# Seven contraction blocks of a modulation moved from VectorE to row products on TensorE, in the prologue of a hybrid decoder block

## The chip, the core and the metric

One core of one Trainium2 chip runs the whole kernel. The metric is the device time of one execution in microseconds (us). The kernel before takes 1734.45 us, the median of three runs that lie between 1732.58 and 1735.91 us.

## What is computed

A decoder block for 1024 tokens of width 1024, in float32. The input is normalised by RMS and modulated by a vector computed from a conditioning vector `c`; then come two mixers (a gated convolution and an mLSTM), a merge, an output projection and a SwiGLU feed-forward part. What matters here is the very beginning:

```python
mod = jnp.einsum("bd,de->be", jax.nn.silu(c), w_ada[l]) + b_ada[l]
sh1, sc1, g1, sh2, sc2, g2 = jnp.split(mod[:, None, :], N_MOD, axis=-1)

h = rms_norm(x, norm_mix_g[l]) * (1.0 + sc1) + sh1
proj = jnp.einsum("bsd,de->bse", h, w_in[l]) + b_in[l]
```

So nothing of the first projection can start before `sh1` and `sc1` are there for the channels that it contracts over, and these are two vectors of 1024 sums over 1024 terms each, that is 8 MB of `w_ada`.

## The kernel before

**The main part.** Matrix products are made from float32 numbers split in two: a high part rounded to fp32r (`hh`, `whi`) and the rest (`hl`, `wlo`), so a product is three fp32r products: high by high, high by low, low by high. After the prologue TensorE works through blocks of 128 output channels; line 158 is the product of such a block. VectorE runs convolution taps and splits beside it.

**The prologue** (lines 175 to 380) prepares `hh` and `hl`, the modulated input in transposed form, channels on partitions: eight tiles `hh[k]` and `hl[k]` of 128 channels by 1024 tokens. The steps:

1. SyncE issues the loads, in this order: the input `x` (4 MB), the first group of `w_ada` (`wad[0]`, four pieces of 512 KB), two raw weight matrices of the first two output blocks (`wraw`, 512 KB each), then the other three groups of `w_ada`.
2. Line 235 squares `x` on ScalarE for the RMS, line 244 scales `x`. Line 248 transposes it on TensorE in 16 blocks of four 128x128 pieces: eight channel tiles `k` for the first half of the tokens (q = 0), then eight for the second half (q = 1). A block lands in one of three PSUM buffers, one of the kind `pn` and two of the kind `pc`. Line 251 copies it out to `xT[k]`, by the string `EVAC` either on ScalarE ("a": all eight of the first half, five of the second) or on VectorE ("v": `xT1`, `xT4`, `xT7` of the second half). The next block that uses the buffer has to wait for that copy.
3. The modulation is made in four groups of 256 channels, `g` = 0 to 3. `mod_sums(g)` forms on VectorE, in eight dependent steps (line 275, then line 277 seven times), the sum over the eight blocks `k` of `wad[g][:, k]` times the column `sc_c[:, k]` of silu(c); the result `macc` still has 128 partial sums, on the partitions. `mod_products(g)` (line 283) adds these up on TensorE: four float32 products of a 128x128 piece of `macc` with a column of ones, into the PSUM buffer `pa`.
4. `mod_cols(g)` (lines 292 and 293) makes columns of `sh1` and `G1` from them on ScalarE. Line 297 makes `hh[k]` for the two tiles of the group, line 300 the full-precision value in place, both on ScalarE, and line 336 makes `hl[k]` from the two on VectorE. For the last group VectorE makes the full value itself (line 340).
5. `first_products(g, kind)` (line 308) multiplies the group's two tiles into the first two output blocks `first[0]` and `first[1]`; the split weights of these are `w_first` (`wf` in the profile), split by `split_rest()` with line 148 (high part, ScalarE) and line 149 (low part, VectorE). For a group there are 16 products with `hh` (`kind` 0: high and low weights) and 8 with `hl` (`kind` 1).
6. After the last group, `glu_gate` reads `first[0]` (line 412, ScalarE), and the next output block at line 158 takes over its PSUM buffer. Four transposes of parameter rows (line 125, through the one buffer `pa`) stand on TensorE around the last products.

**What sets the order.** Every engine runs its instructions strictly in the order of its own program. That order is made when the kernel is built, by a scheduler that goes by priorities (the order in the source) and by its own estimate of when each operand will be there. `in_turn` ties down part of it: the groups in the lists `on_v` (VectorE), `on_s` (ScalarE) and `on_t` (TensorE) stay in the order of the list. The two splits of `split_rest()`, and the copies of the first half of the tokens, stand in no such list.

Of the kernel before, what the change touches and what calls it, by code (L numbers as in the profile page):

```python
# [8 lines left out]
F32 = mybir.dt.float32  # L9
F32R = mybir.dt.float32r  # L10
I32 = mybir.dt.int32
AF = mybir.ActivationFunctionType
# [5 lines left out]
KT = 8  # L18
# [18 lines left out]
EVAC = ("aaaaaaaa", "avaavaav")  # L37
KX = 6
MACC = 3
XB = 7  # L40
GLU_B = 1024
Q0, K0, V0, O0 = 2048, 3072, 4096, 5120
# [6 lines left out]
def hybrid_block(ctx: ExitStack, tc: tile.TileContext, x, c, w_ada, b_ada, norm_mix_g, w_in, b_in,  # L49
                 conv_dw_w, conv_dw_b, conv_ln_g, conv_ln_b, w_conv_pw, b_conv_pw, qk_conv_w,  # L50
                 qk_conv_b, mlstm_norm_g, w_out, norm_ffn_g, w_ffn_up, w_ffn_down, final_norm_g, out):
    nc = tc.nc
# [11 lines left out]
    def ps_mm():  # L64
        return ps.tile([128, 2, 512], F32, name="mm", bufs=2)

    def ps_a():
        return ps.tile([128, 512], F32, name="pa", bufs=1)

    def ps_n():  # L70
        return ps.tile([128, 512], F32, name="pn", bufs=1)

    def ps_c():
        return ps.tile([128, 512], F32, name="pc", bufs=2)
# [20 lines left out]
    ones_col = const.tile([128, 1], F32, name="ones_col")  # L95
# [56 lines left out]
    HALVES = ((0, 512), (512, 1024))  # L152
# [17 lines left out]
    def flat(t):  # L170
        return t.rearrange("p a b -> p (a b)")
# [6 lines left out]
    hh = [big.tile([128, S], F32R, name=f"hh{k}", tag="xa") for k in range(KT)]  # L178
# [5 lines left out]
    pro = prologue.enter_context(tc.tile_pool(name="pro", bufs=1, reuse_waits="tile"))  # L184
    rows = pro.tile([128, 8, 128], F32, name="rows", tag="rows", bufs=2)
    param_columns(param_rows(1, [("c", as_rows(c, 8), 8)], rows[:, 0]))
    sc_c = const.tile([128, KT], F32, name="sc_c")
# [6 lines left out]
    wad = []  # L194
# [35 lines left out]
    rstd = pro.tile([128, 3, 8], F32, name="rstd")  # L230
    xT = [big.tile([128, S], F32, name=f"xT{k}", tag="xb") if k < XB else pro.tile([128, S], F32, name=f"xT{k}") for k in range(KT)]
    for q in range(2):
# [12 lines left out]
        for k in range(KT):  # L245
            p = ps_n() if k % 3 == 0 else ps_c()
# [3 lines left out]
            e = "s" if EVAC[q][k] == "a" else "v"  # L250
            ins = nc.scalar.activation(h, p, AF.Copy) if e == "s" else nc.vector.tensor_copy(h, p)
# [18 lines left out]
    def mod_sums(g):  # L270
        acc = pro.tile([128, 2, 256], F32, name="macc", tag="macc", bufs=MACC)
        parts = [[], []]
        for k in range(KT):
            if k < 1:
                ins = nc.vector.tensor_scalar(acc, wad[g][:, k], sc_c[:, k:k + 1], None, op0=OP.mult)
            else:
                ins = nc.vector.scalar_tensor_tensor(acc, wad[g][:, k], sc_c[:, k:k + 1], acc, op0=OP.mult, op1=OP.add)
            parts[k // 4].append(ins)
        return acc, parts

    def mod_products(g, acc):
        p = ps_a()
        out = [nc.tensor.matmul(p[:, i:i + 1], acc[:, i // 2, (i % 2) * 128:(i % 2) * 128 + 128], ones_col, start=True, stop=True)
               for i in range(4)]
        return p, out

    def mod_cols(g, p):
# [14 lines left out]
    def first_products(g, kind):  # L302
        ks = (2 * g, 2 * g + 1)
        x = hl if kind else hh
        steps = [(i, k, n) for n in ((0,) if kind else (0, 1)) for k in ks for i in range(2)]
        if g == 3 and kind:
            steps.sort(key=lambda step: step[0])
        return [nc.tensor.matmul(flat(first[i])[:, a:b], w_first[i][n][:, k, :], x[k][:, a:b],
                                 start=(g == 0 and k == 0 and n == 0 and not kind), stop=(g == 3 and k == KT - 1 and kind == 1))
                for i, k, n in steps for a, b in HALVES]  # L310

    on_v, on_s, on_t = [], [], []
    w_next = [None]
    hl = []
    acc, parts = mod_sums(0)
    on_v.append(parts[1])
    on_v.append(late_evac["v"])
    on_s.append(late_evac["s"])
    split_rest()
    p, ins = mod_products(0, acc)  # L320
    for g in range(4):
        on_s.append(mod_cols(g, p))
        ks = (2 * g, 2 * g + 1)
# [3 lines left out]
        if g < 3:  # L327
            acc, parts = mod_sums(g + 1)
            on_v += parts
        else:  # L330
            w_next[0] = wp.tile([128, KT, 128], F32R, name="whi", tag="whi"), wp.tile([128, KT, 128], F32R, name="wlo", tag="wlo")
            raw_next = load_raw(win, 0, KT, GLU_B + 128)
# [12 lines left out]
        if g == 2:  # L345
# [10 lines left out]
            bif = const.tile([128, 8], F32, name="bif")  # L356
            nc.sync.dma_start(bif, bass.AP(tensor=b_in.tensor, offset=b_in.offset + IF0, ap=[[0, 128], [1, 8]]))
        on_t.append(first_products(g, 0))
        if g < 3:
            p, ins = mod_products(g + 1, acc)  # L360
            on_t.append(ins)
        on_t.append(first_products(g, 1))
    for groups in (on_v, on_s, on_t):
        in_turn([x for x in groups if x])
# [400 lines left out]
    def chain(*gens):  # L765
        for g in gens:
            yield from g
# [168 lines left out]
    p = ps_a()  # L936
# [25 lines left out]
    def kx(name):  # L962
        return up_.tile([128, D], F32, name=name, tag="kx", bufs=KX)
# [236 lines left out]
    steps = chain(*(w_out_part(q, eh, xs, ss, banks(n)) for n, (q, eh, xs, ss) in  # L1200
                    enumerate(((0, 0, xs0, ss0), (0, 1, xs0, ss0), (1, 0, xs1, ss1), (1, 1, xs1, ss1)))))
# [84 lines left out]
    for gidx, nf in enumerate(groups):  # L1286
# [4 lines left out]
        for t in range(8):  # L1291
# [3 lines left out]
            if gidx < 3:  # L1295
                p = ps_mm()
# [40 lines left out]
```

## Time and profile before

| | before |
|---|---|
| median of three runs | 1734.45 us |
| the profiled execution: its time, and the span from its first instruction to its last | 1735.88 us, 1734.1 us |
| TensorE busy | 1692.9 us, 98% of the span |
| TensorE weight loads | 1418.6 us, 82% |
| VectorE busy | 1249.7 us, 72% |
| ScalarE busy | 611.7 us, 35% |
| GpSimd busy | 52.7 us, 3% |

Times in the rows are counted from the start of the span. PE is TensorE, PEld its weight loads, DVE VectorE, ACT ScalarE, POOL GpSimd, SP SyncE. A row of the timeline gives start, duration, engine, line and operation, out<-in, shapes and a count; several instructions of one kind in succession are one row, and the duration is then that of all. The bracket at the end is idle time of the engine just before, and what ended it.

### The profile page before, as it was taken

To read this page: it belongs to the slowest core of one execution; us is meant where nothing else is said; L and a number is where in the kernel's file an instruction comes from. 1 tells how busy PE (TensorE), PEld (TensorE's weight loads), DVE (VectorE), ACT (ScalarE), POOL (GpSimd) and SP (SyncE) were. 2 spreads that over 40 slices of the span, in tenths; PEclk is the share of its full clock that TensorE was granted. 3 is DMA by queue.
4 is the path that set the end of the run, shared out by engine and by line. 5 is a ranking of instruction groups with operands and counts; after the bars stand their busy time and mean duration, and the time that the engine had idled before them with its cause. 6 is when DMAs were issued, how large, how long until landed. Compare 5 with 4: busy or idle time off the path is not lost. (4 is left out here: it accounts for less than half of the span.)

```text
span 1734.1 us, 20875 instructions
## 1 busy us (share of the span) xinstructions
PE 1692.9 (98%) x8360; PEld 1418.6 (82%) x8360; DVE 1249.7 (72%) x1681; ACT 611.7 (35%) x809; POOL 52.7 (3%) x113
## 2 busy tenths in 40 slices
PE   5999999999999999999999998999999999999998
PEld 4788889888988888888888778888888888778887
DVE  6989998997799669446798668766666665685243
ACT  7424335323433253223522386322222222232122
POOL 0000001000001000000000000000000000000000
PEclk9999999999999999999999999999999999999999
DMA  9221120221111112243694743322222222653121
GB/s 320 63 62 49 37 71 28 61 73 49 37 49 61 61 49 61 73 146 98 209 376 167 230 152 104 98 86 85 86 73 75 84 81 96 226 168 101 58 94 52
DMA packets 194711, 179.91 MB, mean 104 GB/s; under 512 B 7463, under 2 KB 166711, under 8 KB 194615
## 3 DMA queue, kind: packets, MB, share of 16 engines
q1 hardware_dynamic: 177367, 146.61, 27.4%
q10 hardware_dynamic: 17248, 31.99, 5.0%
q8 instruction: 65, 1.06, 0.3%
q14 instruction: 31, 0.25, 0.0%
HBM read 146.06 MB, written 32.51 MB: 103 GB/s over the span
## 5 line engine op out<-in xcount | busy, mean ns | idle before, releaser
L388 DVE SCALAR_TENSOR_TENSOR cacc<-a,col,cacc 128x1024 f32<-128x1024 f32 x240 | 306.8, 1286 | 3.9 <-ACT cacc L386 1.4
L158 PE MATMUL mm<-hh,wlo 128*128 128x512 f32 x864 | 271.2, 391 | 1.5 <-DVE wlo L149 1.5
L158 PE MATMUL mm<-hl,whi 128*128 128x512 f32 x864 | 272.5, 392 | 0.0
L158 PE MATMUL mm<-hh,whi 128*128 128x512 f32 x864 | 271.6, 392 | 0.0
L158 PEld LDWEIGHTS mm<-hh,wlo 128*128 128x128 f32 x864 | 160.3, 188 | 33.6 <-DVE wlo L149 2.7
L158 PEld LDWEIGHTS mm<-hl,whi 128*128 128x128 f32 x864 | 161.0, 188 | 32.1 <-issue 0.5
L158 PEld LDWEIGHTS mm<-hh,whi 128*128 128x128 f32 x864 | 160.5, 188 | 31.6
L148 ACT ACTIVATE whi<-wraw 128x1024 fp32r<-128x1024 f32 x61 | 64.7, 1061 | 226.5 <-PE mm L158 171.3
L149 DVE TENSOR_TENSOR wlo<-wraw,whi 128x1024 fp32r<-128x1024 f32 x61 | 74.5, 1222 | 28.7 <-ACT whi L148 25.2
L1114 PE MATMUL mm<-Bh,gh 128*128 128x512 f32 (+1 forms) x192 | 71.5, 375 | 2.9 <-ACT gh L1051 1.5
L1115 PE MATMUL mm<-Bl,gh 128*128 128x512 f32 (+1 forms) x192 | 71.5, 373 | 0.6 <-DVE Bl L1033 0.6
L604 PE MATMUL mm<-wlo,hh 128*128 128x256 f32 x256 | 72.0, 282 | 0.0
L1116 PE MATMUL mm<-Bh,gl 128*128 128x512 f32 (+1 forms) x192 | 71.2, 371 | 0.0
L1303 DVE TENSOR_TENSOR x<-x,mm 128x1024 f32<-128x1024 f32 x24 | 29.3, 1219 | 52.0 <-PE mm L1301 49.6
L1179 ACT ACTIVATE whi<-wraw 128x512 fp32r<-128x512 f32 (+2 forms) x32 | 25.3, 792 | 114.8 <-PE mm L1301 75.8
L535 DVE SCALAR_TENSOR_TENSOR cacc<-qkraw,col,cacc 128x1024 f32<-128x1024 f32 x48 | 61.5, 1282 | 4.9 <-ACT cacc L533 4.5
L603 PE MATMUL mm<-whi,hh 128*128 128x256 f32 x192 | 54.6, 284 | 0.0
L605 PE MATMUL mm<-whi,hl 128*128 128x256 f32 x192 | 54.2, 283 | 0.0
L1299 PE MATMUL mm<-fa,whi 128*128 128x512 f32 x128 | 50.6, 396 | 1.6 <-DVE cu L1142 0.9
L1300 PE MATMUL mm<-fa,wlo 128*128 128x512 f32 x128 | 50.5, 395 | 1.2 <-DVE wlo L1180 1.2
L1301 PE MATMUL mm<-fa,whi 128*128 128x512 f32 x128 | 50.6, 395 | 0.0
L1052 DVE TENSOR_TENSOR ul<-uraw,uh 128x1024 fp32r<-128x1024 f32 x20 | 24.5, 1225 | 35.4 <-ACT uh L1051 35.4
(444 smaller groups left out, 3893.1 us busy)
## 6 DMA issues: line engine op xcount, KB each, us to landing
wraw<-in_w_in_dram SPq DMA_DIRECT2D x64, 512.0 KB
awt<-in_w_ada_dram SPq DMA_DIRECT2D x32, 512.0 KB
graw<-in_w_ffn_up_dram SPq DMA_DIRECT2D x24, 512.0 KB
uraw<-in_w_ffn_up_dram SPq DMA_DIRECT2D x22, 512.0 KB
draw<-in_w_ffn_down_dram SPq DMA_DIRECT2D x22, 512.0 KB
act_d<-cg ACTq DMA_DIRECT2D x38, 256.0 KB
wad<-in_w_ada_dram SPq DMA_DIRECT2D x16, 512.0 KB
wraw<-in_w_out_dram SPq DMA_DIRECT2D x16, 512.0 KB
```

Source lines behind the costliest of these rows:

```text
L148: nc.scalar.activation(hi, raw, AF.Copy)
L149: (eng or nc.vector).tensor_sub(lo, raw, hi.bitcast(F32))
L158: nc.tensor.matmul(flat(acc)[:, a:b], lhs[:, k, :], rhs[k][:, a:b], start=(first and k == 0), stop=(last and k == kt - 1))
L388: nc.vector.scalar_tensor_tensor(acc, a[:, j:j + S], dw_col(j, ct), acc, op0=OP.mult, op1=OP.add)
L535: nc.vector.scalar_tensor_tensor(cv, raw[:, j:j + S], wcol(j), cv, op0=OP.mult, op1=OP.add)
L603: nc.tensor.matmul(o, hh[k][:, ts_], his[k], start=False, stop=False)
L604: nc.tensor.matmul(o[:, 0:256], hh[k][:, ts_], los[k], start=False, stop=False)
L605: nc.tensor.matmul(o, hl[k][:, ts_], his[k], start=False, stop=(k == KT - 1))
L1114: nc.tensor.matmul(o, a, rh, start=(k == 0), stop=False)
L1115: nc.tensor.matmul(o, a, rl, start=False, stop=False)
L1116: nc.tensor.matmul(o, b, rh, start=False, stop=(k == 3))
L1299: nc.tensor.matmul(o, hi[:, i, :], his[i][:, a:b], start=(i == 0), stop=False)
```

## The change

`ROWS = (3, 4, 0, 0)` gives for each group the number of contraction blocks that leave VectorE. For these blocks TensorE multiplies directly: the column `sc_c[:, k]` is the stationary operand and the 512 numbers per partition of `wad[g][:, k]` are the moving one, so that a float32 product of 1x512 adds up the partitions at once, in one PSUM row (`pa` for group 0, a `pc` buffer for group 1). ScalarE copies the row to SBUF (new line 281). `mod_products` then needs, for each of the four pieces, one more product that turns a piece of the row into a column (new line 299), which the old product with ones (new line 300) adds to. VectorE has five blocks left in group 0 and four in group 1. Group 1's row products are tied into the order of TensorE, and its copy into that of ScalarE; group 0's are not.

`first_products` hands out the last group's 24 products in another order of the source: first those with high parts, without the low weights of the second block; then the `hl` products of the first block; then the rest of the second block.

```diff
+ROWS = (3, 4, 0, 0)
...
     def mod_sums(g):
         acc = pro.tile([128, 2, 256], F32, name="macc", tag="macc", bufs=MACC)
         parts = [[], []]
-        for k in range(KT):
-            if k < 1:
+        row, ins = None, []
+        if ROWS[g]:
+            p = (ps_c() if g else ps_a())[0:1, :]
+            for k in range(ROWS[g]):
+                ins.append(nc.tensor.matmul(p, sc_c[:, k:k + 1], wad[g][:, k].rearrange("p i e -> p (i e)"),
+                                            start=(k == 0), stop=(k == ROWS[g] - 1)))
+            row = pro.tile([1, 512], F32, name="macc", tag="macc", bufs=MACC)
+            copied = nc.scalar.activation(row, p, AF.Copy)
+            (on_t if g else []).append(ins)
+            (on_s if g else []).append([copied])
+        for k in range(ROWS[g], KT):
+            if k == ROWS[g]:
...
-    def mod_products(g, acc):
+    def mod_products(g, sums):
+        acc, row = sums
         p = ps_a()
-        out = [nc.tensor.matmul(p[:, i:i + 1], acc[:, i // 2, (i % 2) * 128:(i % 2) * 128 + 128], ones_col, start=True, stop=True)
-               for i in range(4)]
+        out = []
+        for i in range(4):
+            o = p[:, i:i + 1]
+            if row is not None:
+                out.append(nc.tensor.matmul(o, row[:, i * 128:(i + 1) * 128], ones_col[0:1, :], start=True, stop=False))
+            out.append(nc.tensor.matmul(o, acc[:, i // 2, (i % 2) * 128:(i % 2) * 128 + 128], ones_col, start=row is None, stop=True))
         return p, out
...
-        steps = [(i, k, n) for n in ((0,) if kind else (0, 1)) for k in ks for i in range(2)]
-        if g == 3 and kind:
-            steps.sort(key=lambda step: step[0])
+        steps = [(i, k, n, x) for n in ((0,) if kind else (0, 1)) for k in ks for i in range(2)]
+        if g == 3:
+            if not kind:
+                return []
+            high = [(i, k, n, hh) for n in (0, 1) for k in ks for i in range(2) if n == 0 or i == 0]
+            steps = high + [s for s in steps if s[0] == 0] + [(1, k, 1, hh) for k in ks] + [s for s in steps if s[0] == 1]
```

Three places in the programs that the engines get show what the builder makes of it. First ScalarE, from the scaling of the last part of `x` to the second-half copies, before; `xT4` to `xT7` with the sources `pc_194` to `pc_212` are the last four copies of the first half, `wf00` and `wf10` the splits of the two raw matrices:

```order
L242 ACTIVATE xt3_110<-xt3_110,rstd_147 128x1024
L251 ACTIVATE xT3_151<-pn_188 128x512
L251 ACTIVATE xT4_152<-pc_194 128x512
L251 ACTIVATE xT5_153<-pc_200 128x512
L251 ACTIVATE xT6_154<-pn_206 128x512
L251 ACTIVATE xT7_155<-pc_212 128x512
L148 ACTIVATE wf00_124<-wraw_126 128x1024
L251 ACTIVATE xT0_148<-pn_232 128x512
L148 ACTIVATE wf10_128<-wraw_130 128x1024
L251 ACTIVATE xT2_150<-pc_244 128x512
```

The same place now, where `macc_291` is the row of group 0:

```order
L243 ACTIVATE xt3_110<-xt3_110,rstd_147 128x1024
L252 ACTIVATE xT3_151<-pn_188 128x512
L149 ACTIVATE wf00_124<-wraw_126 128x1024
L281 ACTIVATE macc_291<-pa_287 1x512
L149 ACTIVATE wf10_128<-wraw_130 128x1024
L252 ACTIVATE xT4_152<-pc_194 128x512
L252 ACTIVATE xT5_153<-pc_200 128x512
L252 ACTIVATE xT6_154<-pn_206 128x512
L252 ACTIVATE xT7_155<-pc_212 128x512
L252 ACTIVATE xT0_148<-pn_232 128x512
L252 ACTIVATE xT2_150<-pc_244 128x512
```

Both splits and the copy of the row now stand ahead of four copies that they followed. On VectorE, in the same stretch, the low part of the first split (`wf01`, which needs `wf00`) now comes ahead of all sums of group 0, and the second one behind the first of them; before, they stood behind the sixth and the seventh of eight. The next place on ScalarE is that of the first two `hh` tiles; before, from there to the columns of group 1:

```order
L297 ACTIVATE hh0_82<-xT0_148,sh1_91,G1_90 128x1024
L297 ACTIVATE hh1_83<-xT1_149,sh1_91,G1_90 128x1024
L300 ACTIVATE xT0_148<-xT0_148,sh1_91,G1_90 128x1024
L300 ACTIVATE xT1_149<-xT1_149,sh1_91,G1_90 128x1024
L292 ACTIVATE sh1_91<-pa_341,mod_b_282 128x1
```

And now, where `macc_325` is the row of group 1:

```order
L313 ACTIVATE hh0_82<-xT0_148,sh1_91,G1_90 128x1024
L313 ACTIVATE hh1_83<-xT1_149,sh1_91,G1_90 128x1024
L281 ACTIVATE macc_325<-pc_320 1x512
L316 ACTIVATE xT0_148<-xT0_148,sh1_91,G1_90 128x1024
L316 ACTIVATE xT1_149<-xT1_149,sh1_91,G1_90 128x1024
```

The copy of group 1's row stands ahead of the two full-precision tiles. On TensorE the three row products of group 0 come behind the transposes of channel tile 3 of the first half, one of the four products with its row comes alone behind those of tile 6, and the other seven small products of the group follow the last transposes; the four row products of group 1 come right behind these, ahead of the first product with `hh0`. Last, the end of the prologue on TensorE, from the second tile `hh7` on, before (`mm_280` is `first[0]`, `mm_281` is `first[1]`):

```order
L308 MATMUL mm_280<-hh6_88,wf01_125 128x512 x2
L308 MATMUL mm_281<-hh6_88,wf11_129 128x512 x2
L308 MATMUL mm_280<-hh7_89,wf01_125 128x512 x2
L308 MATMUL mm_281<-hh7_89,wf11_129 128x512 x2
L308 MATMUL mm_280<-hl6_475,wf00_124 128x512 x2
L308 MATMUL mm_281<-hl6_475,wf10_128 128x512 x2
L308 MATMUL mm_280<-hl7_476,wf00_124 128x512 x2
L308 MATMUL mm_281<-hl7_476,wf10_128 128x512 x2
```

And now:

```order
L327 MATMUL mm_280<-hh6_88,wf01_125 128x512 x2
L327 MATMUL mm_280<-hh7_89,wf01_125 128x512 x2
L327 MATMUL mm_281<-hh6_88,wf11_129 128x512 x2
L327 MATMUL mm_281<-hh7_89,wf11_129 128x512 x2
L327 MATMUL mm_280<-hl6_489,wf00_124 128x512 x2
L327 MATMUL mm_281<-hl6_489,wf10_128 128x512 x2
L327 MATMUL mm_280<-hl7_490,wf00_124 128x512 x2
L327 MATMUL mm_281<-hl7_490,wf10_128 128x512 x2
```

Only two pairs of products with `hh` have changed places; the eight with `hl` stand as they stood.

More of the change, by code (lines that the diff above doesn't have):

```diff
@@ L278, in mod_sums @@
             parts[k // 4].append(ins)
-        return acc, parts
-    def mod_products(g, acc):
+        return (acc, row), parts
+    def mod_products(g, sums):
+        acc, row = sums
         p = ps_a()
-        out = [nc.tensor.matmul(p[:, i:i + 1], acc[:, i // 2, (i % 2) * 128:(i % 2) * 128 + 128], ones_col, start=True, stop=True)
-               for i in range(4)]
+        out = []
[4 more added lines that the diff above has]
+            out.append(nc.tensor.matmul(o, acc[:, i // 2, (i % 2) * 128:(i % 2) * 128 + 128], ones_col, start=row is None, stop=True))
         return p, out
@@ L304, in first_products @@
         x = hl if kind else hh
-        steps = [(i, k, n) for n in ((0,) if kind else (0, 1)) for k in ks for i in range(2)]
-        if g == 3 and kind:
-            steps.sort(key=lambda step: step[0])
+        steps = [(i, k, n, x) for n in ((0,) if kind else (0, 1)) for k in ks for i in range(2)]
[4 more added lines that the diff above has]
+            steps = high + [s for s in steps if s[0] == 0] + [(1, k, 1, hh) for k in ks] + [s for s in steps if s[0] == 1]
         return [nc.tensor.matmul(flat(first[i])[:, a:b], w_first[i][n][:, k, :], x[k][:, a:b],
-                                 start=(g == 0 and k == 0 and n == 0 and not kind), stop=(g == 3 and k == KT - 1 and kind == 1))
-                for i, k, n in steps for a, b in HALVES]
+                                 start=(g == 0 and k == 0 and n == 0 and x is hh),
+                                 stop=(g == 3 and k == KT - 1 and x is hl))
+                for i, k, n, x in steps for a, b in HALVES]
     on_v, on_s, on_t = [], [], []
```

## The prediction

> **What bounds the kernel now.** I read the page first, then busy time by stretch, then the timeline of the prologue. The page's first lines and three stretches (up to the first product with `hh`, the rest of the prologue, everything behind it; the columns are length, busy time and count of PE, PEld, DVE, ACT and POOL, granted clock, DMA share, GB/s):
>
> ```profile
> span 1734.1 us, 20875 instructions
> 0.00:30.88 30.88, 11.70 (x74) 8.98 (x74) 18.29 (x39) 22.98 (x41) 2.74 (x8) 0.99 1.00 333
> 30.88:61.59 30.71, 29.90 (x124) 22.77 (x125) 28.75 (x36) 21.65 (x29) 0.22 (x2) 0.90 0.55 161
> 61.59:1734.10 1672.51, 1651.31 (x8163) 1386.83 (x8162) 1202.71 (x1607) 567.05 (x740) 49.74 (x103) 1.00 0.31 98
> ```
>
> Behind 61.59 TensorE is busy for 1651.31 of 1672.51 us. Nothing there is touched, so I take it as a block that starts later or earlier as a whole: the change is worth what it does to 61.59, where line 158 begins. Here is the chain that leads there:
>
> ```profile
> 16.75 1.06 ACT L251 ACTIVATE xT<-pc 128x512 f32<-128x512 f32 x2
> ...
> 17.40 1.12 PE L248 MATMUL pc<-ident,xt 128*128 128x128 f32 x8
> ...
> 18.76 0.58 ACT L251 ACTIVATE xT<-pn 128x512 f32<-128x512 f32 x1
> ...
> 20.67 0.62 ACT L251 ACTIVATE xT<-pc 128x512 f32<-128x512 f32 x1
> ...
> 21.57 1.06 ACT L148 ACTIVATE wf<-wraw 128x1024 fp32r<-128x1024 f32 x1 [0.29 <-DMA wraw<-in_w_in_dram]
> ...
> 22.72 0.69 DVE L251 COPY xT<-pc 128x512 f32<-128x512 f32 x1
> ...
> 23.35 1.06 ACT L148 ACTIVATE wf<-wraw 128x1024 fp32r<-128x1024 f32 x1 [0.23 <-DMA wraw<-in_w_in_dram]
> 23.46 0.42 PEld L248 LDWEIGHTS pc<-ident,xt 128*128 128x128 f32 x4 [1.70 <-DVE xT L251]
> ...
> 24.32 0.58 ACT L251 ACTIVATE xT<-pc 128x512 f32<-128x512 f32 x1
> ...
> 26.29 0.66 PE L248 MATMUL pc<-ident,xt 128*128 128x128 f32 x4 [0.20 <-ACT xT L251]
> ...
> 27.71 1.05 PE L283 MATMUL pa<-ones_col,macc 128*128 128x1 f32 x8 [0.77 <-DVE macc L277]
> ...
> 28.77 0.48 DVE L275 TENSOR_SCALAR macc<-wad,sc_c 128x512 f32<-128x512 f32 x1
> 28.80 0.26 ACT L292 ACTIVATE sh<-pa,mod_b 128x1 f32<-128x1 f32 x1 [2.07 <-PE pa L283]
> ...
> 29.29 5.48 DVE L277 SCALAR_TENSOR_TENSOR macc<-wad,sc_c,macc 128x512 f32<-128x512 f32 x7
> ...
> 29.58 2.38 ACT L297 ACTIVATE hh<-xT,sh,G 128x1024 fp32r<-128x1024 f32 x2
> 30.88 6.74 PE L308 MATMUL mm<-hh,wf 128*128 128x512 f32 x16 [2.12 <-ACT hh L297]
> 31.85 2.38 ACT L300 ACTIVATE xT<-xT,sh,G 128x1024 f32<-128x1024 f32 x2
> ...
> 34.68 2.55 DVE L336 TENSOR_TENSOR hl<-xT,hh 128x1024 fp32r<-128x1024 f32 x2
> ...
> 37.46 0.95 PE L283 MATMUL pa<-ones_col,macc 128*128 128x1 f32 x8
> ...
> 44.52 0.95 PE L283 MATMUL pa<-ones_col,macc 128*128 128x1 f32 x8
> ...
> 51.43 2.55 DVE L336 TENSOR_TENSOR hl<-xT,hh 128x1024 fp32r<-128x1024 f32 x2
> ...
> 51.58 1.04 PE L283 MATMUL pa<-ones_col,macc 128*128 128x1 f32 x8
> ```
>
> From 28.77 on VectorE goes through sums and `hl` without a gap, and at 51.58 the last group's small products begin right behind its last sum. So VectorE's queue sets the end: a delay or gain at its first `hl` (34.68) arrives at 51.58 and at the end. TensorE reaches that point only just before: groups 1 and 2 start their small products at 37.46 and 44.52, 7.06 apart, and a third step gives 51.58 again. The two bounds meet there, so both must move for a gain. The 16 products from 30.88 took 6.74 us, at half clock as shown below.
>
> **What VectorE saves.** Seven of its steps take 5.48 us, 0.78 each. Group 0 loses three (2.3 us), group 1 four (3.1). That is the whole gain on offer, 5.5 us, if nothing else moved.
>
> **What ScalarE pays, group 0.** The first split waits for its raw matrix, which comes at 21.57: ScalarE had been idle for 0.29 then, having finished the four copies ahead of it. Those copies now stand behind both splits. ScalarE will be through with the copy of 18.76 at 19.34, stand still for 2.2 us, split at 21.57, copy the row and split again at 23.35, when the second matrix is there. The loads and their order are unchanged, so I leave both landings where they are. At 24.32 ScalarE thus has nine copies left where it had four.
>
> From there I follow the queues, 0.05 us for a hand-over (22.72 + 0.69 = 23.41, next engine 23.46), 0.48 from copy to copy (two in 1.06, one in 0.58), 0.66 for a block of transposes, 0.46 to 0.5 from one block to the next (two in 1.12, of which the second takes 0.66, leave 0.46). The copies of `xT4` to `xT7` start at 24.3, 24.8, 25.3 and 25.75. That of `xT4` frees at 24.9 the buffer that `xT7`'s transposes need. The second half then goes in rounds of copy, hand-over, transposes: `xT0` is copied at 26.6, `xT2` at 27.1, `xT3` at 28.15, `xT5` at 28.6, and the last transposes, which wait for that buffer, run from 29.3 to 29.9. They ran from 26.29 to 26.95. So they end 3.0 later. VectorE, whose first split waits for ScalarE's at 22.6, has its five sums by 29.2: the three steps saved end as waiting, and no later than the transposes.
>
> The three row products of group 0 run from about 17.4 (0.87 us each, by the next paragraph) to 20.0, ahead of the transposes of `xT4` to `xT6`, which are then through by 21.5; over long before 24.9, they cost nothing. Seven small products of the eight follow the last transposes. Four took 1.05 us, so seven take 1.84: from about 29.8 (29.3 + 0.5) to 31.6, against 28.76 before, 2.84 us later.
>
> **What the rows of group 1 pay.** No row shows a float32 product with one column as weights. The nearest are the float32 products of line 832, 128x512, one instruction of the program in two passes:
>
> ```profile
> L832 PE MATMUL pn<-t4b,ones_d x2: 590/590/591, 792.4 to 792.8; 128*128 128x512 f32 x2
> L832 PE MATMUL pc<-t4b,ones_d x2: 592/592/592, 793.3 to 793.7; 128*128 128x512 f32 x2
> ```
>
> Both start twice, 0.4 us apart, and the second product follows the first by 0.9. As the moving side is the same here, I take 0.87 a product; a lower bound is half of that, one pass instead of two, an upper one twice. Four in a row take 3.5 us and 0.15 to finish. They start at 31.6, right behind the small products, and end at 35.2. The first products with `hh` (ready at 33.7) wait for them until 35.0. ScalarE has `hh0` and `hh1` ready at 34.8, waits for the row, copies it for 0.48 and begins the full value of `xT0` at 35.7. That is ready at 37.0, and the first `hl` starts at 37.05 instead of 34.68: 2.37 later. VectorE has had the four sums of group 1 since 34.5 and waits 2.5 us: the saving of 3.1 ends as waiting too. At half the price `hl` starts at 36.5 since `hh1` and the copy still stand ahead, at twice the price at 40.5.
>
> **TensorE's side.** From 35.0 the 16 products take 3.8 us at full clock instead of 6.6, which ends them at 38.7. The eight small products of group 1 take 2.0 instead of 0.95, to 40.7, against 38.41: 2.3 later. So both chains arrive at the last group's products about 2.3 us late, and the full clock, 2.8 us, goes into paying the start.
>
> **The last group's order.** It buys nothing as built: the products with `hl` stand where they stood, so `first[0]` is ready just as late. Nor would an earlier one give much:
>
> ```profile
> 60.42 1.11 ACT L412 ACTIVATE t<-mm,col 128x1024 f32<-128x1024 f32 x1 [1.41 <-PE mm L308]
> ...
> 61.33 0.33 PE L125 MATMUL pa<-ident,rows 128*128 128x128 f32 x1 [0.38 <-DVE col L128]
> 61.59 0.73 PE L158 MATMUL mm<-hh,whi 128*128 128x512 f32 x2
> ```
>
> Line 158 waits for the read of `first[0]` until 61.53, but the last transpose of parameter rows, ahead of it in the queue, waits for its own buffer until 61.33. That is late next, about 0.1 us on. The swapped `hh` pairs cost nothing.
>
> **The sum.** 0 (VectorE's steps, all turned into waiting) + 2.37 (first `hl`) + 0 (last group) = +2.3 us, rounded down since the small waits of TensorE before the last group may shrink. The profiled execution takes 1735.88 us, its span 1734.1 and 1.78 around it: it becomes 1738.2. The median of the runs shown, 1734.45, is 1.43 lower; I forecast the same step on it: 1736.8. What a measurement of this kernel can tell from no change is about 0.2%, 3.5 us. So this is within it.
>
> **Rival one, the slower side: the clock falls.** Here are stretches of 3.4 us around the place where it did, and the transposes before and after it first rose:
>
> ```profile
> 19.90:23.30 3.40, 2.10 (x18) 1.65 (x16) 3.29 (x5) 2.93 (x5) 0.00 (x0) 1.00 1.20 298
> ...
> 26.70:30.10 3.40, 1.30 (x11) 0.97 (x9) 3.33 (x7) 1.33 (x6) 0.00 (x0) 1.00 1.09 347
> 30.10:33.50 3.40, 2.62 (x6) 2.14 (x7) 3.26 (x5) 3.40 (x4) 0.00 (x0) 0.51 1.09 348
> 33.50:36.90 3.40, 3.40 (x9) 2.62 (x9) 3.26 (x4) 0.72 (x1) 0.00 (x0) 0.50 1.10 350
> ...
> 15.29 0.63 PE L248 MATMUL pc<-ident,xt 128*128 128x128 f32 x2
> 16.90 0.66 PE L248 MATMUL pn<-ident,xt 128*128 128x128 f32 x4 [0.98 <-ACT xT L251]
> ```
>
> TensorE busy for 1.30 of 3.40 us was followed by half clock, for about 7 us; busy for 2.10 it was not. In the new order TensorE is idle from 21.5 (its transposes of `xT6`) to 24.95, but for one small product at 23.2. A stretch from 19.9 has 1.75 busy, between the two rows; one that begins between 20.5 and 22.5 has under 1.3. If the clock falls there, transposes go two in 0.63 as at 15.29, instead of four in 0.66. A round of the second half then costs 0.4 more: three rounds on the path at half clock add 1.1, five of them and slow small products 2.5 to 3. That gives +3.4 to +5.3, 1738.9 in the middle (+4.5). It decides if the fall comes before about 27. The Trainium skill says, on its page "TensorE: Matmul & The Clock Gate", Part 1, that the gate looks at free-running windows of 3.4 us and halves the clock after an idle one. By that rule the fall depends on where the windows lie in each execution, so some would have it and others not; that a window with 1.30 busy was enough here is this trace's number, not the page's. The page's Part 4 says that transposes do not count as activity; by that the gap would be certain to end in a fall. The trace speaks against it: the clock rose between 15.29 and 16.90, when TensorE had run almost nothing but transposes. I give it 0.36.
>
> **Rival two, a row product costs twice my price.** The 3.5 us of group 1 become 7 and lie on the path whole: +5.8 by the first `hl`, 1740.2. Line 832 speaks against it. 0.06.
>
> **Rival three, the wait on ScalarE does not come.** If the raw matrices came some 2 us earlier than in the trace, the transposes would end near 27.5, the small products at 29.2, and the first `hl` start at 34.7: 1734.4, no change. For a gain over 3.5 us the rows of group 1 would have to be nearly free as well. Landing times are those of a queue that moves 333 GB/s all through, against it. 0.08, a third of it faster by over 0.2%.
>
> **How the numbers follow.** The forecast has 0.50. Its own range is +1 to +3.5. With rival one's range up to +5.3 and rival three's end below, 1734.0 to 1740.0 leaves out the upper part of rivals one and two and the gain. Within 0.2%: 0.45 of the forecast, 0.03 of rival one, 0.07 of rival three, 0.55. Slower: 0.03 + 0.32 + 0.05 = 0.40. Faster: 0.02 + 0.03 = 0.05.
>
> **What would show it.** Right, if ScalarE's first split has over 2 us of idle time before it, ended by the DMA; if the last transposes end near 29.9, the small products of group 0 near 31.6; if the row products of group 1 take 3.5 us; if VectorE waits over 2 us before the first `hl`; if the granted clock of 30 to 37 is full. Wrong, if the split is not held, if VectorE's sums end last in group 1, or if transposes from 25 on take 0.42 instead of 0.27 us each.

## The result, and the profile after

The changed kernel takes 1743.88 us (median of 6 runs, 1738.98 to 1746.13), the kernel before 1734.05 (6 runs, 1732.58 to 1735.91): a ratio of 1.0052, 95% interval 1.0040 to 1.0064. It is slower by about 9 us, more than the 0.2% that a measurement can tell, and above the range forecast. The profiled execution took 1743.26, its span 1741.5, which is 7.4 more than the span before.

Busy time by stretch of the changed kernel, cut where line 159 begins (line 158 of before); then three windows of 3.4 us in the prologue:

```profile
0.00:66.24 66.24, 51.08 (x228) 34.16 (x228) 42.40 (x67) 45.88 (x71) 2.95 (x10) 0.97 0.73 231
66.24:1741.50 1675.26, 1652.62 (x8163) 1386.58 (x8162) 1202.64 (x1607) 566.08 (x740) 49.62 (x103) 1.00 0.31 98
26.70:30.10 3.40, 3.15 (x27) 2.67 (x25) 3.14 (x6) 2.60 (x5) 0.00 (x0) 1.00 1.09 347
30.10:33.50 3.40, 3.40 (x14) 1.98 (x14) 2.33 (x4) 1.43 (x5) 0.00 (x0) 0.68 1.11 353
33.50:36.90 3.40, 3.40 (x8) 0.56 (x6) 0.86 (x2) 1.72 (x2) 0.00 (x0) 0.82 1.07 347
```

The prologue ends 4.65 later (66.24 for 61.59; +2.3 was forecast), and what follows takes 2.75 longer (1675.26 for 1672.51; 0 was forecast). The clock was not full from 30.1 to 36.9. The timeline of the prologue:

```profile
17.86 4.32 PE L278 MATMUL pa<-wad,sc_c 128*1 128x512 f32 x6
21.48 1.06 ACT L149 ACTIVATE wf<-wraw 128x1024 fp32r<-128x1024 f32 x1 [2.23 <-DMA wraw<-in_w_in_dram]
22.57 1.23 DVE L150 TENSOR_TENSOR wf<-wraw,wf 128x1024 fp32r<-128x1024 f32 x1 [2.88 <-ACT wf L149]
29.17 0.65 PE L249 MATMUL pc<-ident,xt 128*128 128x128 f32 x4
31.96 4.96 PE L278 MATMUL pc<-wad,sc_c 128*1 128x512 f32 x8
36.85 3.92 PE L327 MATMUL mm<-hh,wf 128*128 128x512 f32 x16
38.71 2.55 DVE L356 TENSOR_TENSOR hl<-xT,hh 128x1024 fp32r<-128x1024 f32 x2 [4.31 <-ACT xT L316]
42.87 0.38 PE L300 MATMUL pa<-ones_col,macc 128*128 128x1 f32 x2
66.24 0.50 PE L159 MATMUL mm<-hh,whi 128*128 128x512 f32 x1
```

Two things run as forecast: ScalarE is held for 2.23 us at the first split, and the last transposes end at 29.82 (29.9 forecast). The rows of group 0 don't: they take 4.32 (2.6 forecast), since the trace's clock record has its rise only at 21.09 here (16.48 in before), but the hold covers that. The seven small products of group 0 take from 29.66 to 31.96, 2.30 (1.84 forecast). Then the four rows of group 1 take 4.96 (3.5 forecast), the first `hl` starts at 38.71 (37.05 forecast), and TensorE is through with group 1's small products at 43.25 (40.7 forecast).

Behind the prologue the loss is at two places. Lining up TensorE's products of the two traces one by one, those of the changed kernel start 4.65 later from 70 to 260 us, and 7.3 later from 312 to 850: a step of 2.65. There stand in before, on VectorE and TensorE:

```profile
285.64 0.42 DVE L698 TENSOR_TENSOR num<-num,pn 128x258 f32<-128x258 f32 x1 [1.43 <-PE pn L629]
303.77 1.22 DVE L149 TENSOR_TENSOR wlo<-wraw,whi 128x1024 fp32r<-128x1024 f32 x1
305.04 0.73 PE L158 MATMUL mm<-hh,wlo 128*128 128x512 f32 x2 [0.79 <-DVE wlo L149]
305.62 0.62 PE L158 MATMUL mm<-hh,whi 128*128 128x512 f32 x2
```

and in the changed kernel:

```profile
291.35 0.42 DVE L718 TENSOR_TENSOR num<-num,pn 128x258 f32<-128x258 f32 x1 [1.54 <-PE pn L649]
309.48 1.22 DVE L150 TENSOR_TENSOR wlo<-wraw,whi 128x1024 fp32r<-128x1024 f32 x1
310.75 0.84 PE L159 MATMUL mm<-hh,wlo 128*128 128x512 f32 x2 [1.86 <-DVE wlo L150]
311.39 1.06 PE L159 MATMUL mm<-hh,whi 128*128 128x512 f32 x2
312.25 1.06 PE L159 MATMUL mm<-hl,whi 128*128 128x512 f32 x2
```

VectorE's addition to `num` is 5.71 later than before, 1.06 more than the prologue's shift. The low split, behind it in VectorE's queue, is 5.71 later too, TensorE waits 1.86 instead of 0.79 (+1.07), and behind that wait its pairs of products take 1.06 instead of 0.62 for 3.4 us (+1.6). The second place is at 1500 us, a step of 1.46, with a wait that before doesn't have there:

```profile
1500.91 1.22 DVE L1323 TENSOR_TENSOR x<-x,mm 128x1024 f32<-128x1024 f32 x1 [3.87 <-DMA x<-x_d]
1502.28 0.47 PE L1319 MATMUL mm<-fa,whi 128*128 128x512 f32 x1 [1.24 <-DVE x L1323]
```

Between 1530 and 1550 the profiled execution of before has a loss of its own, 1.8 us against the changed kernel: its granted clock is 0.50 from 1545.66 to 1549.07, which no other trace has there. So the two steps show in the spans only in part.

Why is anything different there? The build's scheduler orders the whole program by its own estimate of times, and the change shifts its prologue. The order of the two programs is equal again behind the prologue but for two places (and a swap of neighbours here and there): the first head of the mLSTM (TensorE's rows around 275 to 300 us) and the start of the feed-forward (1045 to 1066 us). In the first one TensorE has, between about 275 us and the last product into `pn` (line 629 of before), 69 of the value products of lines 601 to 605, where before has 60. Nine products that start 0.12 apart are 1.07 us, which is the delay of `num`.

### The profile page after: what moved, and what is told of

Its sections match the earlier page's. It is cut to its first block, busy times and chain, and to the rows that moved or that the text cites. A ratio compares the mean times of both kernels' runs of the same rounds, so it can differ in the third digit from the quotient of the medians.

```text
span 1741.5 us, 20931 instructions
## 1 busy us (share of the span) xinstructions
PE 1703.7 (98%) x8390; PEld 1420.7 (82%) x8390; DVE 1245.0 (71%) x1674; ACT 612.0 (35%) x811; POOL 52.6 (3%) x113
## 3 DMA queue, kind: packets, MB, share of 16 engines
q8 instruction: 66, 1.08, 0.3%
```

## Experiments

Theory: the prologue loses by what waits behind what in group 0, and by the clock; the rest is order far behind, which no line of the change names. The rivals are in each expectation. The starts and steps of all kernels (block: where the first product of line 158 starts; rows: what group 1's four row products take; ahead: value products more than before ahead of the last `pn`; step: at 300 us against the profiled execution of before; the ratio, with its 95% interval, is to the kernel before as timed beside it, whose median was 1733.46 for e1 to e4, 1733.97 for e5 to e8 and 1734.45 for e9 to e12; a dash where there is none). Block, rows and step are each read from one execution:

| kernel | block | rows | ahead | step | median, ratio |
|---|---|---|---|---|---|
| before | 61.59 | - | 0 | 0 | 1734.05 |
| changed | 66.24 | 4.96 | 9 | 2.65 | 1743.88, 1.0052 |
| e1 | 61.98 | 3.59 | 0 | -0.09 | 1734.09, 1.0007 (0.9997 to 1.0016) |
| e2 | 65.25 | 3.59 | 0 | 0.01 | 1737.74, 1.0027 (1.0017 to 1.0038) |
| e3 | 67.11 | - | 9 | 2.69 | 1739.99, 1.0040 (1.0025 to 1.0055) |
| e4 | 66.80 | - | 2 | 0.29 | 1738.44, one run |
| e5 (changed) | 67.01 | 3.60 | 9 | 2.63 | 1744.42, 1.0061 (1.0047 to 1.0074) |
| e6 | 66.53 | 5.29 | 9 | 2.67 | 1744.01, 1.0059 (1.0043 to 1.0074) |
| e7 | 61.66 | 2.73, three | 0 | -0.03 | 1734.96, 1.0006 (0.9997 to 1.0015) |
| e8 | 67.04 | 3.59 | 9 | 2.67 | 1742.85, one run |
| e9 | 63.09 | 3.59 | 0 | -0.01 | 1736.76, 1.0014 (1.0003 to 1.0024) |
| e10 | 67.83 | 6.36 | -4 | -0.33 | 1744.53, one run |
| e11 | 61.52 | - | 0 | 0.08 | 1734.98, one run |
| e12 | 62.77 | - | 0 | 0.04 | 1734.50, 1.0005 (0.9996 to 1.0014) |

**e1, group 1 alone**

```
-ROWS = (3, 4, 0, 0)
+ROWS = (0, 4, 0, 0)
```

> Only group 1's four row products, their copy and its turned small products; group 0 and ScalarE's order as before, and the order of every engine behind the prologue as before. Theory (half of the cost sits in the prologue, most of it in ScalarE's hold and in row products at half clock; the rest is the order of instructions far behind): without the hold the transposes end at 27.0 as before, the four row products (0.85 to 0.87 each) run from about 28.8 to 32.3, the 16 products with hh start at 32.3 (30.88 before), the first hl at 34.2 (34.68 before), and the small products of group 1 take 2.55 (0.95 before). The block at line 158 of before starts between 61.6 and 63.5, and everything behind it takes the 1672.5 us of before: span +0 to +2. Rival (the row products and the turned small products carry the whole prologue loss of 4.65 us, the hold none): the block starts at 65 to 66, span +4.

```profile
28.74 3.59 PE L278 MATMUL pc<-wad,sc_c 128*1 128x512 f32 x8
32.26 3.92 PE L327 MATMUL mm<-hh,wf 128*128 128x512 f32 x16
34.12 1.23 DVE L356 TENSOR_TENSOR hl<-xT,hh 128x1024 fp32r<-128x1024 f32 x1 [1.78 <-ACT xT L316]
61.98 0.73 PE L159 MATMUL mm<-hh,whi 128*128 128x512 f32 x2
```

As expected, to 0.1 us: rows at 0.87 each, the clock full, `hl` at 34.12. VectorE waits for 1.78 of the 3.1 it saves. Group 1's rows are nearly free and bring nothing (+0.39 at the block). The rest of the prologue loss comes only together with group 0's part.

**e2, copies first**

```
-        nc.scalar.activation(hi, raw, AF.Copy)
+        ins = nc.scalar.activation(hi, raw, AF.Copy)
+        for earlier in behind:
+            queue_behind(ins, earlier)
...
+            if q == 0 and k > 3 and e == "s":
+                early_evac.append(ins)
...
```

`split_rest()` passes `early_evac` as `behind`, and the copy of group 0's row is put behind the same copies.

> The changed kernel with ScalarE's copies of the first transposes held ahead of both high splits and of group 0's row copy, so that nothing of ScalarE waits behind the raw matrix but the splits. By that, the order far behind is that of before but for seven rows of TensorE. Theory: the transposes end at 27.0 to 27.5 in place of 29.82, row products of group 1 follow at 29.3, the first hl starts at 34.4 to 35 (38.71 in the changed kernel), the first block behind the prologue at 62.0 to 63.0 (66.24), and there is no jump at 304 us: span 1734.5 to 1736, some 6 us below the changed kernel's 1741.5. Rival (the hold is hidden, rows carry the cost): the block starts at 65 to 66. Second rival (the far loss is the chip's clock falling by chance and not the order): the jump at 304 us is there again, span 1737 to 1738.

```profile
17.77 4.11 PE L283 MATMUL pa<-wad,sc_c 128*1 128x512 f32 x6
29.26 0.65 PE L252 MATMUL pc<-ident,xt 128*128 128x128 f32 x4
65.25 0.73 PE L161 MATMUL mm<-hh,whi 128*128 128x512 f32 x2
```

A miss on the block. ScalarE is free, and the last transposes still end at 29.91: group 0's row products, 4.11 here since the clock record has its rise only at 20.57, stand ahead of the transposes, and both splits now stand ahead of the second half's copies. My prediction called them free because ScalarE held what follows; they are a second cover of the same length. The far order is that of before, and there is no step.

**e3, columns for group 1.** No rows: `ROWS = (0, 4, 0, 0)` counts blocks that `mod_products` adds as columns:

```
+                for k in range(ROWS[g]):
+                    out.append(nc.tensor.matmul(o, wad[g][:, k, i // 2, (i % 2) * 128:(i % 2) * 128 + 128], sc_c[:, k:k + 1], start=(k == 0), stop=False))
```

> Group 1's four blocks on TensorE as sixteen products of 128 weights by one column of c, added straight into the modulation's columns: no row, no copy, no turn; group 0 and ScalarE as before. Behind the prologue its order is the changed kernel's, row for row but for one product near the start. Theory (far order costs): at about 304 us after the start, plus the prologue's shift, TensorE waits 1.5 to 2 us for the low split of a weight matrix (0.79 in before, 1.86 in the changed kernel), products take twice their time for 3 us after it, and the part behind the prologue takes 2 to 3 us more than the 1672.5 of before. Rival (chance of the clock, or the prologue's own shift): it takes 1672.5 within 0.5. In the prologue: sixteen products more at 0.24 each (four took 0.95) are 3.8 us of TensorE's queue, of which 2 to 3.8 arrive at the first block: 63.5 to 65.5.

```profile
311.61 0.73 PE L159 MATMUL mm<-hh,wlo 128*128 128x512 f32 x2 [1.87 <-DVE wlo L150]
313.40 1.05 PE L159 MATMUL mm<-hh,wlo 128*128 128x512 f32 x2
```

Another prologue, without hold or row, but the changed kernel's far order: the step is there, 2.69, with the same wait and the half speed behind it. Its block is later than expected (67.11): the twenty products of group 1 ran in part at half clock.

**e4, the hold alone.** Before, with the copies behind both splits (`queue_behind(late, ins)` in `load_split` for the same four copies).

> The kernel before with ScalarE's copies of xT4 to xT7 (first half) behind both high splits, as the change has them; no row products, all sums on VectorE. Behind the prologue the order is neither that of before nor quite that of the changed kernel, so only the prologue is read. Theory: the hold alone delays the last transposes from 26.95 to 29.5 to 30, small products of group 0 end at 30.5 to 31 (28.76), the first hl starts 1 to 2.5 us later than 34.68 and the first block at 62.5 to 64. Rival (hidden behind VectorE's queue): the first hl starts at 34.7 to 35 and the block at 61.6 to 62.

```profile
24.92 1.97 PE L251 MATMUL pc<-ident,xt 128*128 128x128 f32 x8 [4.91 <-ACT xT L254]
36.40 5.51 PE L313 MATMUL mm<-hh,wf 128*128 128x512 f32 x16 [2.60 <-ACT hh L302]
```

The hold is not hidden; it costs more than I expected (block 66.80), since TensorE idles for 4.91 us, and its clock falls: eight transposes take 1.97 instead of 1.12. In the changed kernel the row products fill that idle time. Two value products stand ahead, and the step is 0.29.

**e5, the changed kernel again**

> The changed kernel once more, to see what of its trace comes back. Theory (the jump behind the prologue is its order of instructions): TensorE's wait of 1.86 us for a low split near 309 us, the products at half speed behind it and the step of 2.66 at about 300 us are there again, and the wait near 1501 of 1.2 us too; the block behind the prologue starts within 1.5 us of 66.24, by where the clock falls. Rival (chance of this execution): the step at 300 is gone or under 1 us.

```profile
26.76 1.92 PE L249 MATMUL pc<-ident,xt 128*128 128x128 f32 x8
30.63 0.65 PE L249 MATMUL pc<-ident,xt 128*128 128x128 f32 x4
33.19 3.60 PE L278 MATMUL pc<-wad,sc_c 128*1 128x512 f32 x8
311.48 0.73 PE L159 MATMUL mm<-hh,wlo 128*128 128x512 f32 x2 [1.86 <-DVE wlo L150]
```

The waits behind the prologue come back to the hundredth, and the steps (2.63, 1.37). The fall of the clock comes back at another place. Here the clock has its rise at 15.59, group 0's rows take 2.74 instead of 4.32, and in the idle time behind them it falls at 25.83, as rival one of the prediction has it. The transposes then end at 31.28, 1.46 later than in the first execution, and group 1's rows run at full clock, 1.36 shorter. A second fall, at 42.90, is this execution's own, and its block comes 0.77 later. e8 has the same two falls within 0.1 us.

**e6, neither.** e2, and group 0's rows behind the first half's transposes:

```
+            if not g:
+                for i in ins:
+                    queue_behind(i, transposed[-1])
...
```

> The changed kernel with both things of group 0 out of the way: ScalarE's copies of the first transposes ahead of the high splits, and group 0's three row products behind the first half's transposes, with their copy behind the splits. Theory (ScalarE's hold and the row products lie side by side and each alone delays the transposes; with neither the prologue loss goes): row products from about 22 to 24.7, the second half's transposes 1.2 us later than in the first experiment, the block behind the prologue at 63 to 64.5, against 61.98 in the first experiment, 65.25 in the second and 66.24 in the changed kernel. Rival (the turned small products and the row of group 0 carry the loss): 65 or later. Behind the prologue its order is the changed kernel's but for one row of VectorE, so the step of 2.66 us at about 300 us is there; span 1737 to 1739.

```profile
23.06 1.23 DVE L152 TENSOR_TENSOR wf<-wraw,wf 128x1024 fp32r<-128x1024 f32 x1 [3.26 <-ACT wf L149]
29.77 0.38 PE L313 MATMUL pa<-ones_col,macc 128*128 128x1 f32 x2 [0.52 <-DVE macc L301]
31.94 5.29 PE L285 MATMUL pc<-wad,sc_c 128*1 128x512 f32 x8
```

A miss: 66.53. A third queue is held. VectorE stands 3.26 us at the low split (2.88 in the changed kernel), with group 0's sums behind it; before had done five of them by then. And the clock falls on the rows (5.29).

**e7, three rows of group 1**

```
-ROWS = (3, 4, 0, 0)
+ROWS = (0, 3, 0, 0)
```

> Three blocks of group 1 alone as row products, group 0 untouched; behind the prologue the order is that of before but for a few rows. Three products of 0.87 (2.6 us) from 28.75 end at 31.4, about when the first hh value is ready (30.9 in before), VectorE saves 2.3 us, ScalarE's copy of the row stands ahead of the first full value. Theory: the first block starts at 61.0 to 61.8 (61.59 before, 61.98 with four), the time is that of before within 0.1%. Rival (a row saves VectorE more than it costs, as the change assumes): the block starts at 59.5 to 60.5 and the time falls by 1 to 2 us.

The block starts at 61.66; the time is that of before. No version with row products beat it.

**e8, ScalarE's pair put back.** Far behind, the change had also moved one `kh` ahead of the second `Ch`:

```
+                if conv_i == 10:
+                    queue_behind(ins, state_split[2])
```

> The changed kernel with one thing of the far order put back: ScalarE's two values of Ch stand ahead of the four of kh again, as before (they are at about 274 us in before); TensorE still has its value products ahead of the score products there, as in the changed kernel. Theory A (ScalarE's pair makes VectorE late): the step at about 300 us falls from 2.66 to under 1 us. Theory B (TensorE's order does: the products that VectorE waits for come behind the value products): it stays at 2 to 2.7. The prologue is the changed kernel's.

The step stays, 2.67. Theory A falls.

**e11, that pair alone.** The opposite edit in the kernel before: `queue_behind(state_split[2], ins)` for the first `kh`.

> The kernel before with one pair of ScalarE's queue swapped as in the changed kernel (the first kh of head 1 ahead of the second Ch, at about 275 us), TensorE's value products where they were; the prologue is untouched. Theory B of the eighth experiment (TensorE's order makes the step): under 0.7 us at 300. Theory A (ScalarE's pair): 1 to 2.7 us.

No step (0.08). With the table's column: 9 products ahead make 2.63 to 2.69 in five traces of four programs, 2 make 0.29 (2 x 0.12 = 0.24), -4 make -0.33 (read at 305 to 310 us, as e10's order differs again behind), none -0.09 to 0.08. The delay goes by TensorE's order. Half clock is added where the wait is 1.86 us, and not where it is 1.00 (e4), 0.79 or 0.45 (e10).

**e9, three queues.** e6, with group 0's sums ahead of VectorE's splits, and the rows behind the third block of the second half:

```
+        for earlier in sums:
+            queue_behind(ins, earlier)
...
+            if q == 1 and k <= 2:
+                transposed.append(ins)
```

> As the sixth experiment, with VectorE freed as well: its remaining sums of group 0 stand ahead of its low splits (in the changed kernel VectorE waits 2.88 us for the first split with the sums behind it), and group 0's rows come behind the third block of the second half's transposes. Behind the prologue its order is that of before but for a few rows. Theory (group 0's loss is a matter of what waits behind what, plus TensorE's own 2.6 us of rows and 0.8 of turned products ahead of the first products with hh): the block behind the prologue at 64 to 65 instead of 66.53, and no step at 300 us, so the time is 1736 to 1738, some 7 us below the changed kernel. Rival (VectorE's sums were not late): 66 to 66.5 again, time 1738.5.

```profile
22.68 2.73 PE L287 MATMUL pa<-wad,sc_c 128*1 128x512 f32 x6
30.18 3.59 PE L287 MATMUL pc<-wad,sc_c 128*1 128x512 f32 x8
63.09 0.73 PE L163 MATMUL mm<-hh,whi 128*128 128x512 f32 x2
306.54 0.74 PE L163 MATMUL mm<-hh,wlo 128*128 128x512 f32 x2 [0.79 <-DVE wlo L152]
```

The same seven blocks as row products, 7 us faster than the changed kernel: no hold, the clock full, no step. The block comes a little earlier than expected. Its +2.3 us is by chance what the prediction gave for the change: that sum had the hold in it.

**e10, the same with the rows earlier** (`if q == 0` in place of the condition above).

> The same with group 0's rows behind the first half's transposes, where TensorE waits 1.46 us in the first experiment; far behind its order is another again, so only the prologue is read. Theory: half of the rows' 2.6 us falls into that wait; the block starts at 63 to 64.5. Rival: 65 or later, as the small products and the clock go.

```profile
31.19 6.36 PE L287 MATMUL pc<-wad,sc_c 128*1 128x512 f32 x8
```

A miss, 67.83: the rows start 1.0 later than in e9 and take 2.8 longer, as the clock fell at about 30. That I hadn't counted.

**e12, the clock kept.** Before, with two products whose result nobody reads:

```
+        if g == 1:
+            spare = ps_c()[0:1, :]
+            on_t.append([nc.tensor.matmul(spare, sc_c[:, k:k + 1], wad[g][:, k].rearrange("p i e -> p (i e)"),
+                                          start=(k == 0), stop=(k == 1)) for k in range(2)])
```

> The kernel before with two row products more (work added, nobody reads their result) in TensorE's wait of 2.12 us ahead of the first products with hh; all else is before, instruction for instruction. It tells whether VectorE's queue alone sets the end of the prologue. Prediction's view (VectorE's queue and TensorE's both reach 51.58): the clock stays full, the sixteen products take 3.9 in place of 6.74, and the block still starts at 61.3 to 61.7. Rival (TensorE's queue sets the end): it starts at 58.8 to 60, and the time falls by 2 us.

```profile
31.50 4.48 PE L312 MATMUL mm<-hh,wf 128*128 128x512 f32 x16
51.34 2.55 DVE L340 TENSOR_TENSOR hl<-xT,hh 128x1024 fp32r<-128x1024 f32 x2
51.47 1.05 PE L287 MATMUL pa<-ones_col,macc 128*128 128x1 f32 x8 [1.08 <-DVE macc L281]
```

The clock was not kept: it fell at 29.25, for 3.41 us, and the two extra products took 2.97. Still the sixteen take 2.3 us less, group 1's small products start 1.64 earlier (35.82 for 37.46), and TensorE then waits 1.08 for VectorE, which arrives at 51.34 as in before (51.43). VectorE's queue does set that point. The block comes later (62.77): the clock fell again behind that wait, from 53.14 to 56.56.

## Why the prediction was wrong

- **"Nothing there is touched, so I take it as a block that starts later or earlier as a whole"** (of what follows 61.59) is the step that failed worst. The change touches no line there, but the order there. I had compared the two orders in the prologue only. e3, e5, e6 and e8 have the step with the changed order there, e1, e2, e7, e9, e11 and e12 have none with that of before or nearly so: 2.65 us at 300, shown. That TensorE's nine products make it, and not VectorE's order, which has a swap there too, goes by the count and by `num`'s wait for `pn`; no run moved these products alone. The 1.46 at 1500 is read from the wait for `x`; the five traces with the changed order have 1.36 to 1.65 there, e10 has 1.05, e2 and e12, whose order there is that of before or nearly so, have 0.7, the others of that order none. So order alone doesn't make it; how it comes about wasn't tried.
- **The full clock from 30 to 37**, on which the forecast rested, failed, and with it the size of one term: group 1's rows took 4.96, not 3.5. The price of 0.87 each was right (3.59 or 3.60 in five traces). Rival one's +4.5 is near the prologue's +4.65 by luck: it put the fall into the transposes, which is right in e5 and e8 (+5.42 and +5.45) and wrong in this execution, and it went by the busy share, which doesn't tell the fall here, as shown below.
- **The small products**: eight took 2.55, not 2.0 (40.70 to 43.25 by the rows above and 0.31 from one to the next), and group 0's seven 2.30, not 1.84. The price was taken from products that don't alternate with ones of a single row.
- **The first `hl`**, the 2.37 of the sum, came 4.03 later than in before (38.71 for 34.68), as it waits behind group 1's rows and their copy.
- **Slips without effect**: 35.0 and 3.8 make 38.8, not 38.7; the last sum of chances uses 0.35, 0.05 and 0.10 for rivals given as 0.36, 0.06 and 0.08.
- **"They cost nothing"** of group 0's row products holds only while ScalarE is held; e2 shows them ready to take its place. The two claims about VectorE hold: its saving turned into waiting, and its queue set the end of before (e12).
- **Right**: the hold (2.23), the end of the transposes (29.82 for 29.9), the last group's order, which did nothing.

So the prologue's 4.65 is: 0.39 for group 1's rows (e1); 1.1 for group 0's (e9 less e1); 1.8 for the three held queues and 1.4 for the clock (the rows start 1.78 earlier and take 1.37 less in e9 than in the changed kernel). These are differences of single executions, and the 1.8 has group 0's rows at another place in it too. With the steps it is 8.8. The spans of the two profiled executions differ by 7.4, since the fall of before at 1545 takes 1.8 off and small steps between add 0.5. The medians differ by 9.8; 1.0 of that stays open, within the 7 us over which the changed kernel's runs spread.

**Where the clock falls.** Within each trace the granted clock changes only at points that lie whole multiples of 3.41 us apart, and they differ between executions (the changed kernel has one at 31.33, e5 at 32.66). In the prologue it fell in all traces but e1, e2 and e9. Here are stretches between two such points, and the ones behind them: in the changed kernel's prologue, at its wait of 1.86 us, and at the second fall of e5.

```profile
27.92:31.33 3.41, 3.16 (x25) 2.77 (x23) 2.41 (x4) 1.68 (x3) 0.00 (x0) 1.00 1.09 347
31.33:34.74 3.41, 3.41 (x8) 1.07 (x8) 2.74 (x4) 2.67 (x6) 0.00 (x0) 0.50 1.09 350
307.81:311.22 3.41, 1.55 (x8) 0.97 (x7) 3.37 (x5) 2.36 (x3) 0.33 (x1) 1.00 0.00 1
311.22:314.63 3.41, 3.41 (x10) 2.65 (x9) 3.41 (x4) 0.00 (x0) 0.00 (x0) 0.50 0.61 154
39.49:42.90 3.41, 3.41 (x22) 2.84 (x20) 3.23 (x5) 0.19 (x1) 0.00 (x0) 1.00 0.55 162
42.90:46.31 3.41, 3.41 (x10) 2.73 (x11) 3.23 (x6) 3.04 (x6) 0.00 (x0) 0.50 0.07 16
```

So the busy share doesn't tell a fall: 1.55 of 3.41 us had one behind it, and so had 3.16 and 3.41. Those of 3.16 and 3.41, from 27.92 and 39.49, end in strings of small products, which have one moving column each and which the profile counts as busy. e2 and e9 run such strings too and keep the clock, with the points elsewhere. Before and e1 happen to have the same points: from 26.72 to 30.13 before was busy for 1.28 and fell, e1, with row products from 28.74 on, was busy for 2.72 and did not. What counts for the clock wasn't tried, and stays open.

## What to carry to other kernels

Compare the order of the whole program, not only of the part that was edited: where a scheduler orders by estimated times, an edit at the start can move nine products at 280 us and cost 2.7 us at 300. Work that is moved to another engine pays only if the queue it leaves is not held at the same place by something else: take away one hold, and see what the next one is, before calling a step free. Products moved into an idle stretch can keep the clock up (e1) and need not (e12); a wait of 1.1 or 1.9 us elsewhere lost it again.

## What the runs showed of the hardware

- A wait of TensorE of 1.86 us, in a stretch otherwise full (busy 1.55 of 3.41), was followed by half clock for 3.41 us (pairs 1.06 instead of 0.62) in all five traces that have such a wait there; one of 0.79, or of 1.00 in e4, was not. The Trainium skill, on its page "TensorE: Matmul & The Clock Gate", Part 1, tells of a free-running window and of a fall after an idle one. The different places of the fall in two executions of one kernel agree with the first; by the second the clock should have stayed up here, and the measurement decides.
- A float32 product with a single column as weights, 512 wide, takes 0.87 to 0.9 at full clock, as much as one of 128 columns at line 832. A small product takes 0.31 from one to the next where one with a single row of weights alternates with one of 128 rows; four without took 0.95.
